# A hybrid decoder step: the SSD loop traces the next chunk's decays and scaled operands ahead of this chunk's products

## The chip, the cores and the metric

The kernel runs on one core of a Trainium2 chip. The metric is the device time of one execution in microseconds (us), the median of three runs. A TensorE matmul of 32-bit floats with 128 rows appears in the profile as two instructions, and one of the type fp32r as one.

## The reference, cut to what matters

One layer of a decoder: a prompt of 512 tokens and 8 samples of 8 tokens share the weights. A first projection feeds three groups of heads side by side (Mamba-2 SSD, mLSTM, RG-LRU), one output projection merges them, and an MLP follows. The change touches only the SSD heads of the prompt: 16 heads of 64 in 2 groups, with a state of 128, in chunks of 128 tokens that hand a state on.

```python
def ssd_chunked(x, dt, a, bm, cm, s0):
    L = math.gcd(x.shape[1], CHUNK)
    mask = causal_mask(L)[None, :, :, None, None]

    def step(s, inp):
        xc, dtc, bc, cc = inp
        cum = jnp.cumsum(dtc * a, axis=1)
        decay = jnp.exp(jnp.where(mask, cum[:, :, None] - cum[:, None, :], -jnp.inf))
        att = jnp.einsum('btgn,bsgn->btsg', cc, bc)[..., None] * decay
        xdt = xc * dtc[..., None]
        y = (jnp.einsum('btsge,bsgep->btgep', att, xdt)
             + jnp.einsum('btgn,bgepn->btgep', cc, s) * jnp.exp(cum)[..., None])
        xend = xdt * jnp.exp(cum[:, -1:] - cum)[..., None]
        s = jnp.exp(cum[:, -1])[..., None, None] * s + jnp.einsum('bsgn,bsgep->bgepn', bc, xend)
        return s, y
```

Only the two terms that hold the state s depend on the chunk before; att, xdt, xend and the decays of a chunk do not.

## The kernel before

**The main stream.** All large products are done in three passes of fp32r: a weight block of 128 x 1024 (raw) is loaded by SP's queue (L128), split by ScalarE into a high part (wh, L150) and by VectorE into a low part (wl, L151). A unit is 48 matmuls g (L163): 8 slices of the inner dimension, 3 passes, 2 halves of the 576 tokens. Loads run 4 blocks ahead of the units and splits 2 blocks ahead, with 3 buffers for raw and 3 for the split parts. At the end of a unit its result is copied out of PSUM: q, k, v of the mLSTM at L901, convolutions at L610 to L652 (conv steps r at L625 on VectorE, xbc at L650).

**The generators.** All smaller work is written as Python generators: `ssd(g)` for the two SSD groups, `mlstm`, the RG-LRU, `ada_gen` for the modulation (adap L217, adas L227, modt L228). A unit calls `slot()` after every 4 slices and at its end, and each active generator is then advanced to its next `yield`. So a `yield` sets between which g matmuls a piece of work is traced. A scheduler then orders the traced instructions on each engine, by priority in the order of tracing and by when it reckons operands and buffers free; each engine runs its order strictly from front to back. SBUF tiles (`self.T`) come from one pool of 54 buffers, small PSUM tiles (`self.P`) from 4, the PSUM pairs of units from 2.

**A chunk of ssd before** has two pieces with a `yield` behind each.

- The front (L685 to L719): TensorE computes the scores of B and C and transposes B (cb, L687, L688) and the four x tiles (xt, L690). VectorE masks the scores (cbm, L692) and scales x into xdt and xend (L697). The decays: the running sums of the chunk, broadcast over the partitions by a DMA (cumb, L666), less the row's own sum (att, 8 x L706), exponentiated by ScalarE (L708), times the masked scores (L710). From the second chunk on also the exponentials of cumb times C (ce; L713 on ScalarE, L715 on VectorE). At its end the next chunk's two cumb loads are issued.
- The back (L720 to L748): TensorE multiplies att by xdt (py, L728) and the state S by ce into the same PSUM tile (L731), and computes the state's increment (ps, L733). VectorE adds x times a constant (y, L735) and forms the new state (L742; GpSimd multiplies the old one at L739; the first chunk's is a copy by ScalarE, L744).

Behind the four chunks the same generator handles the group's sample tokens (L751 to L848). It starts with loads of cumf and cump (L759, L762) and of states s (L755); exponentials of both follow on ScalarE (L788, L790), then copies of operands on ScalarE (L800, L801) and products pc and pu (L821, L828).

Of the kernel before, what the change touches and what calls it, by code (L numbers as in the profile page):

```python
# [25 lines left out]
AF = mybir.ActivationFunctionType  # L26
# [41 lines left out]
class Kernel:  # L68
# [601 lines left out]
    def ssd(self, g):  # L670
        nc, io = self.nc, self.io
# [6 lines left out]
        for i in range(4):  # L678
            self.y[4 * g + i] = ys[i]
        mask = self.v("mask")  # L680
        S = None
        cums = [self.ssd_cum(g, 0, h) for h in range(2)]
        yield
        for c in range(4):
            tok = slice(c * 128, (c + 1) * 128)  # L685
            p1, p2 = self.P("cb"), self.P("xt")
            nc.tensor.matmul(p1[:, :128], B[:, tok], Cc[:, tok], start=True, stop=True)  # L687
            nc.tensor.transpose(p1[:, 128:256], B[:, tok], self.ident)  # L688
            for i in range(4):
                nc.tensor.transpose(p2[:, i * 128:(i + 1) * 128], xs[i][:, tok], self.ident)  # L690
            cb = self.T("cbm")
            nc.vector.tensor_tensor(cb[:, :128], p1[:, :128], mask, op=OP.mult)  # L692
            nc.scalar.activation(cb[:, 128:256], p1[:, 128:256], AF.Copy)
            hh = slice(g * 8, g * 8 + 8)
            xdt, xend = self.T("xdt"), self.T("xend")
            for dst, q in ((xdt, 64), (xend, 96)):
                nc.vector.tensor_tensor(dst[:, :512].rearrange("p (h d) -> p h d", h=8),  # L697
                                        p2.rearrange("p (h d) -> p h d", h=8),
                                        self.col1[:, c, q + g * 8:q + g * 8 + 8][:, :, None].to_broadcast([128, 8, 64]),
                                        op=OP.mult)  # L700
            att, ce = [], []
            for h2 in range(2):
                E = self.T("att")
                for h in range(4):
                    hd = g * 8 + h2 * 4 + h
                    self.eng("att").tensor_scalar(E[:, h * 128:(h + 1) * 128], cums[h2][:, h * 128:(h + 1) * 128],  # L706
                                            self.col1[:, c, hd:hd + 1], 0.0, op0=OP.add, op1=OP.min)
                nc.scalar.activation(E[:, :512], E[:, :512], AF.Exp)  # L708
                e3 = E[:, :512].rearrange("p (h t) -> p h t", h=4)
                self.eng("attm").tensor_tensor(e3, e3, cb[:, None, :128].to_broadcast([128, 4, 128]), op=OP.mult)  # L710
                att.append(E)
                if c:
                    nc.scalar.activation(cums[h2][:, :512], cums[h2][:, :512], AF.Exp)  # L713
                    c3 = cums[h2][:, :512].rearrange("p (h t) -> p h t", h=4)
                    self.eng("ce").tensor_tensor(c3, c3, Cc[:, None, tok].to_broadcast([128, 4, 128]), op=OP.mult)  # L715
                    ce.append(cums[h2])
            if c < 3:
                cums = [self.ssd_cum(g, c + 1, h) for h in range(2)]
            yield  # L719
            py, pst = self.P("py"), self.P("ps")  # L720
            for i in range(4):
                for step in range(2 if c else 1):
                    for j in range(2):
                        h = 2 * i + j
                        o = py[64 * j:64 * j + 64, i * 128:(i + 1) * 128]
                        hs = slice((h % 4) * 128, (h % 4 + 1) * 128)
                        if step == 0:
                            nc.tensor.matmul(o, xdt[:, h * 64:(h + 1) * 64], att[h // 4][:, hs], start=True,  # L728
                                             stop=not c)
                        else:  # L730
                            nc.tensor.matmul(o, S[:, h * 64:(h + 1) * 64], ce[h // 4][:, hs], start=False,  # L731
                                             stop=True)
            nc.tensor.matmul(pst, cb[:, 128:256], xend[:, :512], start=True, stop=True)  # L733
            for i in range(4):
                nc.vector.scalar_tensor_tensor(ys[i][:, tok], xs[i][:, tok], self.v("ssdd")[:, 4 * g + i:4 * g + i + 1],  # L735
                                               py[:, i * 128:(i + 1) * 128], op0=OP.mult, op1=OP.add)
            Sn = self.T("S")
            if c:
                self.eng("S").tensor_tensor(Sn[:, :512].rearrange("p (h d) -> p h d", h=8),  # L739
                                        S[:, :512].rearrange("p (h d) -> p h d", h=8),  # L740
                                        self.decb[:, hh, c][:, :, None].to_broadcast([128, 8, 64]), op=OP.mult)
                nc.vector.tensor_tensor(Sn[:, :512], Sn[:, :512], pst, op=OP.add)  # L742
            else:
                nc.scalar.activation(Sn[:, :512], pst, AF.Copy)  # L744
            S = Sn
            if c == 3:
                self.queue("ssm_p").dma_start(io["ssm_p"][g], S[:, :512])
            yield  # L748
# [8 lines left out]
        tok = slice(TP, NT)  # L757
# [13 lines left out]
        cb = self.T("cbm")  # L771
# [6 lines left out]
        xdt, xend = self.T("xdt"), self.T("xend")  # L778
# [27 lines left out]
        for i in range(4):  # L806
            for j in range(2):
                h = 2 * i + j
# [829 lines left out]
```

## Time and profile before

| what | us |
|---|---|
| median of 3 runs (lowest, highest) | 988.71 (987.87, 989.5) |
| the profiled execution, its own time | 991.71 |
| its span | 989.9 |

The mean granted TensorE clock of the profiled execution is 0.987 of full speed. The two SSD groups lie at 119 to 178 us and at 197 to 286 us of the span, their prompt chunks at 119 to 170 and 203 to 251. Rows of a timeline give the start in us, the duration in us, the engine and line, what is written and read, and in brackets how long the engine stood idle before it and what ended that. Durations of neighbours overlap a little, because an instruction is issued before the one ahead of it has drained; so the time that one takes up on its engine is read from the difference of two starts.

### The profile page before, as it was taken

To read this page: it belongs to the slowest core of one execution; us is meant where nothing else is said; L and a number is where in the kernel's file an instruction comes from. 1 tells how busy PE (TensorE), PEld (TensorE's weight loads), DVE (VectorE), ACT (ScalarE), POOL (GpSimd) and SP (SyncE) were. 2 spreads that over 40 slices of the span, in tenths; PEclk is the share of its full clock that TensorE was granted. 3 is DMA by queue.
4 is the path that set the end of the run, shared out by engine and by line. 5 is a ranking of instruction groups with operands and counts; after the bars stand their busy time and mean duration, and the time that the engine had idled before them with its cause. 6 is when DMAs were issued, how large, how long until landed. Compare 5 with 4: busy or idle time off the path is not lost.

```text
span 989.9 us, 18136 instructions
## 1 busy us (share of the span) xinstructions
PE 959.0 (97%) x7370; PEld 904.9 (91%) x7370; DVE 579.1 (59%) x1206; ACT 400.4 (40%) x741; POOL 134.9 (14%) x194
## 2 busy tenths in 40 slices
PE   8899879999899999999999999999999999999996
PEld 4789868888788889998999999999999999999996
DVE  4669878687877586557444455533553355335544
ACT  3455734554656674436222243312431144114320
POOL 2811210420331222010000000000000000000032
PEclk9999989999999999999999999999999999999998
DMA  9722263764653424434333212222222222222202
GB/s 345 294 86 79 77 177 128 236 192 140 199 196 116 151 89 138 136 124 162 109 110 108 98 65 86 85 86 77 74 85 85 86 85 83 74 79 86 86 22 96
DMA packets 51218, 119.61 MB, mean 121 GB/s; under 512 B 6956, under 2 KB 17468, under 8 KB 51136
## 3 DMA queue, kind: packets, MB, share of 16 engines
q1 hardware_dynamic: 47024, 111.06, 33.3%
q10 hardware_dynamic: 3744, 6.85, 1.8%
q8 instruction: 58, 0.95, 0.4%
q0 software_dynamic: 368, 0.55, 0.2%
q14 instruction: 24, 0.20, 0.1%
HBM read 108.68 MB, written 9.76 MB: 120 GB/s over the span
## 4 chain that ended last, share of the span: by engine, by line
PE 84%; DVE 4%; ACT 3%; DMA 2%; issue 1%; POOL 0%; POOLq 0%; DVEq 0%; SPq 0%; ACTq 0%
PE g L163 73%; PE adap L217 1%; PE g L1363 1%; PE ps L733 1%; PE py L728 1%; DMA nmb<-scr_nm 1%; PE py L731 1%; DMA ada<-ada 1%; DMA cump<-scr_cum 0%; PE lg L1129 0%; PE xt L690 0%; PE adas L227 0%; DVE wl L151 0%; PE pu L828 0%; PE pn L970 0%
## 5 line engine op out<-in xcount | busy, mean ns | idle before, releaser
L150 ACT ACTIVATE wh<-raw 128x1024 fp32r<-128x1024 f32 x123 | 130.0, 1058 | 343.8 <-PE g L163 321.3
L151 DVE TENSOR_TENSOR wl<-raw,wh 128x1024 fp32r<-128x1024 f32 x123 | 151.3, 1231 | 43.2 <-ACT wh L150 37.8
L163 PE MATMUL g<-hnh,wh 128*128 128x288 f32 x688 | 155.6, 304 | 9.7 <-ACT r L613 5.2
L163 PE MATMUL g<-hnh,wl 128*128 128x288 f32 x688 | 153.0, 301 | 0.4 <-DVE wl L151 0.4
L163 PE MATMUL g<-hnl,wh 128*128 128x288 f32 x688 | 151.7, 300 | 0.0
L163 PEld LDWEIGHTS g<-hnh,wh 128*128 128x128 f32 x688 | 112.1, 191 | 19.1 <-ACT r L613 6.3
L163 PEld LDWEIGHTS g<-hnh,wl 128*128 128x128 f32 x688 | 112.4, 191 | 2.9 <-issue 1.5
L163 PEld LDWEIGHTS g<-hnl,wh 128*128 128x128 f32 x688 | 112.5, 191 | 1.9 <-issue 1.7
L163 PE MATMUL g<-h2h,wh 128*128 128x288 f32 (+1 forms) x512 | 111.2, 298 | 0.0
L163 PE MATMUL g<-h2l,wh 128*128 128x288 f32 (+1 forms) x512 | 111.1, 298 | 0.0
L163 PE MATMUL g<-h2h,wl 128*128 128x288 f32 (+1 forms) x512 | 110.4, 297 | 0.0
L163 PE MATMUL g<-hh,wl 128*128 128x288 f32 x480 | 102.7, 295 | 0.0
L163 PE MATMUL g<-hh,wh 128*128 128x288 f32 x480 | 102.7, 295 | 0.0
L163 PE MATMUL g<-hl,wh 128*128 128x288 f32 x480 | 102.6, 295 | 0.0
L306 DVE SCALAR_TENSOR_TENSOR xr<-g,modt,xr 128x288 f32<-128x288 f32 x38 | 19.7, 518 | 141.2 <-PE g L163 141.2
L163 PEld LDWEIGHTS g<-h2l,wh 128*128 128x128 f32 x512 | 83.7, 189 | 0.0
L163 PEld LDWEIGHTS g<-h2h,wl 128*128 128x128 f32 x512 | 83.6, 189 | 0.0
L163 PEld LDWEIGHTS g<-h2h,wh 128*128 128x128 f32 x512 | 83.0, 188 | 0.1
L163 PEld LDWEIGHTS g<-hh,wl 128*128 128x128 f32 x480 | 77.0, 188 | 0.0
L163 PEld LDWEIGHTS g<-hl,wh 128*128 128x128 f32 x480 | 76.9, 188 | 0.0
L163 PEld LDWEIGHTS g<-hh,wh 128*128 128x128 f32 x480 | 76.8, 188 | 0.0
L1405 POOL TENSOR_SCALAR xr<-xr,vec 128x576 f32<-128x576 f32 (+2 forms) x8 | 15.2, 1904 | 384.8 <-ACT sqa L1237 364.4
(398 smaller groups left out, 1523.7 us busy)
## 6 DMA issues: line engine op xcount, KB each, us to landing
raw<-w SPq DMA_DIRECT2D x124, 512.0 KB, 3.5
ada<-ada SPq DMA_DIRECT2D x32, 512.0 KB, 5.1
ada<-ada SPq DMA_DIRECT2D x32, 256.0 KB, 5.8
cumb<-scr_cum SPq DMA_DIRECT2D x16, 256.0 KB, 5.8
s<-s SPq DMA_DIRECT2D x16, 256.0 KB, 4.6
ssm_s<-s ACTq DMA_DIRECT2D x16, 256.0 KB, 4.2
x<-x SPq DMA_DIRECT2D x8, 288.0 KB, 5.2
xr<-x SPq DMA_DIRECT2D x8, 288.0 KB, 3.9
```

Of the source, the lines that this page charges most:

```text
L150: nc.scalar.activation(hi, raw, AF.Copy)
L151: nc.vector.tensor_tensor(lo, raw, hi.bitcast(FT), op=OP.subtract)
L163: self.nc.tensor.matmul(pg.h[h][:m, :e], w(k), xx[:, h * HALF:h * HALF + e], start=start and n == 0, stop=stop and n == 2)
L217: nc.tensor.matmul(ps[32 * j:32 * j + 32, :256], self.cs[:, k, :], ks(k), start=k < 4, stop=k >= 4)
L306: self.nc.vector.scalar_tensor_tensor(dst[:, :HALF], pg.h[0][:, :HALF], gate[:, 0:1], x[:, :HALF], op0=OP.mult, op1=OP.add)
L728: nc.tensor.matmul(o, xdt[:, h * 64:(h + 1) * 64], att[h // 4][:, hs], start=True, stop=not c)
L731: nc.tensor.matmul(o, S[:, h * 64:(h + 1) * 64], ce[h // 4][:, hs], start=False, stop=True)
L733: nc.tensor.matmul(pst, cb[:, 128:256], xend[:, :512], start=True, stop=True)
L1363: nc.tensor.matmul(pgs[i].h[p][:, :c.stop - c.start], w(k), xs[k][x][:, c], start=k == 0 and j == 0, stop=k == 7 and j == 2)
L1405: self.eng("fin").tensor_scalar(x, x, self.v("fnw")[:, o:o + 1], None, op0=OP.mult)
```

## The change

The front becomes a function `front(c)` that returns its tiles, the back a function `back(c, S, ops)`. The order in which they are traced, `|` standing for a `yield`, was f0 | b0 | f1 | b1 | f2 | b2 | f3 | b3 and is now f0 | f1 | b0 | f2 | b1 | f3 | b2 | b3. The number of yields is the same, so what follows in the generator is traced in the same slot as before; f1 to f3 come one slot earlier and b0 to b2 one slot later. The next chunk's cumb loads are issued at the end of each front as before, and so one slot earlier. No instruction is added, removed or changed. Lines from L687 on carry numbers in the new kernel that are 1 to 16 higher (L728 is L734, L710 is L711, L735 is L741, L759 is L775); the text names lines by the kernel before.

```diff
-        S = None
-        cums = [self.ssd_cum(g, 0, h) for h in range(2)]
-        yield
-        for c in range(4):
+        cums = {0: [self.ssd_cum(g, 0, h) for h in range(2)]}
+        hh = slice(g * 8, g * 8 + 8)
+
+        def front(c):
...
             if c < 3:
-                cums = [self.ssd_cum(g, c + 1, h) for h in range(2)]
-            yield
+                cums[c + 1] = [self.ssd_cum(g, c + 1, h) for h in range(2)]
+            return cb, xdt, xend, att, ce
+
+        def back(c, S, ops):
+
+            cb, xdt, xend, att, ce = ops
+            tok = slice(c * 128, (c + 1) * 128)
             py, pst = self.P("py"), self.P("ps")
...
-            S = Sn
+            return Sn
+
+        yield
+        S = None
+        ready = [front(0)]
+        yield
+        for c in range(4):
+            if c < 3:
+                ready.append(front(c + 1))
+                yield
+            S = back(c, S, ready.pop(0))
             if c == 3:
                 self.queue("ssm_p").dma_start(io["ssm_p"][g], S[:, :512])
             yield
```

What the scheduler makes of it is seen at three places. First TensorE's order just ahead of chunk 1's first product in the first group, before (xt_1487 are chunk 1's transposed x tiles, py_1434 and py_1563 the products of chunks 0 and 1, g_1724 a unit):

```order
L690 MATMUL xt_1487<-vec,xbc_918 128x128
L690 MATMUL xt_1487<-vec,xbc_1005 128x128
L163 MATMUL g_1724<-hnl_576,wh_1458 128x288 x2
L163 MATMUL g_1724<-hnh_575,wl_1459 128x288 x2
L163 MATMUL g_1724<-hnh_616,wh_1458 128x288
L728 MATMUL py_1434<-att_1379,xdt_1368 64x128 x4
L163 MATMUL g_1724<-hnh_616,wh_1458 128x288
L163 MATMUL g_1724<-hnl_617,wh_1458 128x288 x2
L163 MATMUL g_1724<-hnh_616,wl_1459 128x288 x2
L728 MATMUL py_1563<-att_1501,xdt_1497 64x128 x2
L733 MATMUL ps_1564<-xend_1498,cbm_1494 128x512
```

and now (xt_1564 are chunk 2's, py_1631 chunk 1's product, g_1731 the same unit):

```order
L691 MATMUL xt_1564<-vec,xbc_918 128x128
L691 MATMUL xt_1564<-vec,xbc_1005 128x128
L163 MATMUL g_1731<-hnl_576,wh_1478 128x288 x2
L163 MATMUL g_1731<-hnh_575,wl_1479 128x288 x2
L163 MATMUL g_1731<-hnh_616,wh_1478 128x288 x2
L163 MATMUL g_1731<-hnl_617,wh_1478 128x288 x2
L163 MATMUL g_1731<-hnh_616,wl_1479 128x288 x2
L734 MATMUL py_1631<-att_1449,xdt_1445 64x128 x2
L739 MATMUL ps_1632<-xend_1446,cbm_1442 128x512
L737 MATMUL py_1631<-cumb_1386,S_1521 64x128 x2
```

Before, 10 g matmuls stand between chunk 1's own transposes and its product; now chunk 2's transposes are there, and chunk 1's stand further ahead: behind them come 32 g matmuls of the same unit, chunk 0's products, chunk 2's cb pair and 5 more g matmuls, none of which is in these rows.

Second, VectorE's order at the same place, before, from the last y of chunk 0 on (cbm_1494, xdt_1497, att_1501 and att_1510 are chunk 1's):

```order
L735 SCALAR_TENSOR_TENSOR y_1310<-xbc_1005,vec,py_1434 128x128
L692 TENSOR_TENSOR cbm_1494<-cb_1486,vec 128x128
L697 TENSOR_TENSOR xdt_1497<-xt_1487,col_1216 128x512
L697 TENSOR_TENSOR xend_1498<-xt_1487,col_1216 128x512
L706 TENSOR_SCALAR att_1501<-cumb_1386,col_1216 128x128 x4
L706 TENSOR_SCALAR att_1510<-cumb_1388,col_1216 128x128 x4
L650 SCALAR_TENSOR_TENSOR xbc_1560<-r_1547,r_1553 128x512
L652 SCALAR_TENSOR_TENSOR xbc_1560<-r_1547,r_1553 128x64
L151 TENSOR_TENSOR wl_1849<-raw_1590,wh_1848 128x1024
L710 TENSOR_TENSOR att_1501<-att_1501,cbm_1494 128x512
```

and now, from chunk 1's xdt on (xdt_1445, att_1449 and att_1458 are chunk 1's, y chunk 0's results):

```order
L697 TENSOR_TENSOR xdt_1445<-xt_1435,col_1216 128x512
L697 TENSOR_TENSOR xend_1446<-xt_1435,col_1216 128x512
L707 TENSOR_SCALAR att_1449<-cumb_1386,col_1216 128x128 x4
L151 TENSOR_TENSOR wl_1735<-raw_1476,wh_1734 128x1024
L707 TENSOR_SCALAR att_1458<-cumb_1388,col_1216 128x128 x4
L625 SCALAR_TENSOR_TENSOR r_1553<-r_1547,cwh,r_1553 128x600
L741 SCALAR_TENSOR_TENSOR y_1307<-xbc_752,vec,py_1506 128x128
L741 SCALAR_TENSOR_TENSOR y_1308<-xbc_840,vec,py_1506 128x128
L741 SCALAR_TENSOR_TENSOR y_1309<-xbc_918,vec,py_1506 128x128
L741 SCALAR_TENSOR_TENSOR y_1310<-xbc_1005,vec,py_1506 128x128
L711 TENSOR_TENSOR att_1449<-att_1449,cbm_1442 128x512
```

Chunk 1's scaled operands and decays stood behind chunk 0's y and now stand ahead of them; only the masking (L710, now L711) is still behind. Ahead of the second of these pieces, behind the common L228, stand only chunk 1's mask of cb, chunk 0's two maskings and a step L625.

Third, SP's queue of loads in the second group, before (nmb, c: an mLSTM head's; cumf, cump and s: the sample tokens'; raw_3195 and raw_3381: weight blocks):

```order
L128 DMA raw_3025<-w 128x1024
L666 DMA cumb_2661<-scr_cum 128x4x128
L666 DMA cumb_2663<-scr_cum 128x4x128
L908 DMA nmb_2722<-scr_nm 128x576
L911 DMA c_455_2724<-c 128x520
L911 DMA c_456_2725<-c 128x520
L128 DMA raw_3195<-w 128x1024
L237 DMA ada_2959<-ada 128x1024
L237 DMA ada_2961<-ada 128x1024
L128 DMA raw_3381<-w 128x1024
L759 DMA cumf_2963<-scr_cum 64x8x64
L762 DMA cump_2964<-scr_cum 64x4x64 x2
```

and now:

```order
L128 DMA raw_3025<-w 128x1024
L128 DMA raw_3195<-w 128x1024
L924 DMA nmb_2729<-scr_nm 128x576
L927 DMA c_459_2731<-c 128x520
L927 DMA c_460_2732<-c 128x520
L237 DMA ada_2959<-ada 128x1024
L237 DMA ada_2961<-ada 128x1024
L775 DMA cumf_2963<-scr_cum 64x8x64
L778 DMA cump_2964<-scr_cum 64x4x64 x2
L771 DMA s_495_2968<-s 128x512
L771 DMA s_496_2970<-s 128x512
```

The weight load raw_3195 now stands ahead of nmb instead of behind it, chunk 3's cumb pair further ahead, and raw_3381 no longer stands between the modulation's loads and cumf; it now follows four s loads.

More of the change, by code (lines that the diff above doesn't have):

```diff
@@ L693, in ssd @@
             nc.scalar.activation(cb[:, 128:256], p1[:, 128:256], AF.Copy)
-            hh = slice(g * 8, g * 8 + 8)
             xdt, xend = self.T("xdt"), self.T("xend")
@@ L701, in ssd @@
             att, ce = [], []
+            cu = cums.pop(c)
             for h2 in range(2):
@@ L705, in ssd @@
                     hd = g * 8 + h2 * 4 + h
-                    self.eng("att").tensor_scalar(E[:, h * 128:(h + 1) * 128], cums[h2][:, h * 128:(h + 1) * 128],
+                    self.eng("att").tensor_scalar(E[:, h * 128:(h + 1) * 128], cu[h2][:, h * 128:(h + 1) * 128],
                                             self.col1[:, c, hd:hd + 1], 0.0, op0=OP.add, op1=OP.min)
@@ L712, in ssd @@
                 if c:
-                    nc.scalar.activation(cums[h2][:, :512], cums[h2][:, :512], AF.Exp)
-                    c3 = cums[h2][:, :512].rearrange("p (h t) -> p h t", h=4)
+                    nc.scalar.activation(cu[h2][:, :512], cu[h2][:, :512], AF.Exp)
+                    c3 = cu[h2][:, :512].rearrange("p (h t) -> p h t", h=4)
                     self.eng("ce").tensor_tensor(c3, c3, Cc[:, None, tok].to_broadcast([128, 4, 128]), op=OP.mult)
-                    ce.append(cums[h2])
+                    ce.append(cu[h2])
             if c < 3:
-                cums = [self.ssd_cum(g, c + 1, h) for h in range(2)]
-            yield
+                cums[c + 1] = [self.ssd_cum(g, c + 1, h) for h in range(2)]
[3 more added lines that the diff above has]
+            tok = slice(c * 128, (c + 1) * 128)
             py, pst = self.P("py"), self.P("ps")
```

## Prediction

> **What bounds the kernel now.** I read the page's busy table first, then who waited for whom on TensorE, then the stretches around the long waits, then the timeline there.
>
> ```profile
> PE 959.0 (97%) x7370; PEld 904.9 (91%) x7370; DVE 579.1 (59%) x1206; ACT 400.4 (40%) x741; POOL 134.9 (14%) x194
> ```
>
> TensorE is busy for 97% of the span, so an edit that removes no matmul can win only what is left: its waits, and stretches in which its clock is lowered. The change moves work only around the SSD chunks (119 to 260 us), so I list the waits of that time and shortly behind it. Columns: total us, times, longest.
>
> ```profile
> PE py L728 <- DVE att L710: 6.2, 2, 5.8
> PE g L163 <- ACT v L901: 1.3, 1, 1.3
> PE pu L828 <- DVE modt L228: 1.2, 1, 1.2
> PE pc L821 <- PE g L163: 0.6, 1, 0.6
> PE pu L828 <- DVE c L1028: 0.6, 1, 0.6
> ```
>
> One wait of 5.8 us stands out: a product of a chunk (py, L728) waits for the masked decays of that chunk (att, L710). The stretches of 2 us show what it costs besides; columns: us, PE busy (instructions), granted clock, DMA share, GB/s.
>
> ```profile
> 140.00:142.00 2.00, 0.00 (x0) 0.66 0.00 0
> 142.00:144.00 2.00, 1.46 (x5) 0.50 0.44 125
> 144.00:146.00 2.00, 2.00 (x7) 0.50 0.99 307
> 146.00:148.00 2.00, 2.00 (x22) 0.63 0.54 98
> ...
> 266.00:268.00 2.00, 1.47 (x7) 0.74 0.88 299
> 268.00:270.00 2.00, 2.00 (x11) 0.50 0.80 299
> 270.00:272.00 2.00, 2.00 (x20) 0.91 0.65 195
> ```
>
> After the long wait the clock is at half until about 147.5. Lost there from 142 on: 2 x (0.50 + 0.50 + 0.37) = 2.74 us, less half of the 0.54 us in which TensorE still stood: 2.47. A second fall, at 266 to 272, costs 2 x (0.26 + 0.50 + 0.09) = 1.70.
>
> Why the wait arises is in the timeline (start, us, what; in brackets the idle time before).
>
> ```profile
> 124.72 0.51 PE L227 MATMUL adas<-vec,adarow 128*128 128x9 f32 x4
> 128.91 0.17 DVE L228 TENSOR_TENSOR modt<-adas,vec 128x18 f32<-128x18 f32 x1
> 132.08 0.83 DVE L625 SCALAR_TENSOR_TENSOR r<-r,cwh,r 128x600 f32<-128x600 f32 x1
> 135.93 1.12 DVE L735 SCALAR_TENSOR_TENSOR y<-xbc,vec,py 128x128 f32<-128x128 f32 x4 [3.02 <-PE py L728]
> 136.97 0.28 DVE L692 TENSOR_TENSOR cbm<-cb,vec 128x128 f32<-128x128 f32 x1
> 137.17 0.68 DVE L697 TENSOR_TENSOR xdt<-xt,col 128x512 f32<-128x512 f32 x1
> 137.77 0.68 DVE L697 TENSOR_TENSOR xend<-xt,col 128x512 f32<-128x512 f32 x1
> 138.37 1.65 DVE L706 TENSOR_SCALAR att<-cumb,col 128x128 f32<-128x128 f32 x8
> 139.93 0.68 DVE L650 SCALAR_TENSOR_TENSOR xbc<-r,r 128x512 f32<-128x512 f32 x1
> 140.67 1.22 DVE L151 TENSOR_TENSOR wl<-raw,wh 128x1024 fp32r<-128x1024 f32 x1
> 141.81 0.69 DVE L710 TENSOR_TENSOR att<-att,cbm 128x512 f32<-128x512 f32 x1
> 142.54 0.69 PE L728 MATMUL py<-att,xdt 128*64 128x128 f32 x4 [5.81 <-DVE att L710]
> ```
>
> VectorE first stands idle for 3.02 us for chunk 0's products, and only then starts chunk 1's front (mask, xdt, xend, decays). TensorE has five g matmuls left by then and stops at chunk 1's products, with all later g matmuls behind them in its order. One engine waits for the other, in turn.
>
> **The change, part by part.** It adds and removes no instruction; it moves. Four terms.
>
> *Term A, the long wait.* In the new order chunk 1's transposes stand right behind chunk 0's, and 32 g matmuls, chunk 0's products and chunk 2's front come before chunk 1's products. I walk both engines from the last point that both programs share: TensorE behind the adas matmuls (next start 125.05 in the trace), VectorE behind L228 (next start 128.99). These rows of the chain of waits give TensorE's durations.
>
> ```profile
> 61.08 39.55 PE g L163 x286
> 132.22 0.59 PE py L728 x8
> 132.81 1.05 PE ps L733 x2
> 239.09 0.59 PE xt L690 x4
> ```
>
> A g matmul takes 39.55 / 286 = 0.138. TensorE up to chunk 0's products: 47 of these (6.49), the cb pair (no longer than an xt group, 0.59) and xt (0.59): 132.7. On to chunk 1's products: two py groups 1.18, ps 1.05, cb 0.59, 5 g 0.69, xt 0.59, 10 g 1.38: 138.2. VectorE, by differences of the starts above: mask of cb 0.20, two L710 1.20, a convolution step 0.8, xdt and xend 1.20, four L706 0.78, wl 1.14, four L706 0.78, a step 0.8, four y 1.04, L710 0.60: 8.54, so 137.5. The decays are ready 0.7 us before TensorE asks. Walked on in the same way, chunks 2 and 3 have theirs about 3 us ahead. So 5.81 + 2.47 = 8.3 us go. The margin is thin: I put back 1.0, between the ends 0 and 8.3, nearer to 0 because the walk ends on the right side.
>
> What is late next? VectorE. These are its busy times (third figure) in stretches of 10 us, behind PE and PEld.
>
> ```profile
> 80.00:90.00 10.00, 10.00 (x78) 10.00 (x77) 9.76 (x14) 5.50 (x10) 1.21 (x5) 1.00 0.21 67
> ...
> 120.00:130.00 10.00, 10.00 (x87) 9.22 (x87) 9.12 (x22) 6.15 (x14) 1.51 (x5) 1.00 0.87 256
> 130.00:140.00 10.00, 6.74 (x52) 5.36 (x51) 6.98 (x20) 3.25 (x6) 1.06 (x1) 1.00 0.45 133
> 140.00:150.00 10.00, 7.46 (x59) 5.01 (x60) 8.41 (x21) 3.39 (x8) 1.06 (x1) 0.66 0.40 107
> 150.00:160.00 10.00, 10.00 (x89) 8.89 (x89) 7.61 (x24) 2.50 (x7) 1.06 (x1) 1.00 0.75 238
> 160.00:170.00 10.00, 10.00 (x87) 8.53 (x86) 7.99 (x19) 5.32 (x12) 1.27 (x1) 1.00 0.20 79
> ```
>
> From 120 to 170 VectorE has 40.1 us of work, and TensorE without its loss needs 50 - 8.3 = 41.7: VectorE would be 96% busy. That is tight, but from 80 to 90 it is 98% busy while TensorE never stops.
>
> *Term B, the second SSD group.* Its only wait of this kind is the rest of the first row, 6.2 - 5.8 = 0.4; there the new order has whole units between a chunk's front and its products. Gain 0.4 (0 to 0.4).
>
> *Term C, the first mLSTM head.* The 1.2 us wait for modt stands behind the nmb load; order and load stay in step with TensorE's work. Nothing (the ends are -1.2 and +1.2).
>
> *Term D, the second group's sample tokens.* The waits 1.3, 0.6 and 0.6 fall at 262 to 266 and bring on the 1.70 of low clock: 4.2 in all. They end a chain on ScalarE that began late.
>
> ```profile
> 249.14 1.33 SPq L762 DMA_DIRECT2D cump<-scr_cum  x2
> 254.44 0.42 ACT L790 ACTIVATE cump<-cump 128x256 f32<-128x256 f32 x1 [2.66 <-DMA cump<-scr_cum]
> ```
>
> ScalarE stood 2.66 us for cump. In SP's new order cumf and cump no longer stand behind the last weight load (raw), and chunk 3's products, whose tiles they reuse, stand 12 g matmuls (1.7 us) earlier. So most of the 2.66 us can go, and about as much of the waits, which sum to 2.5. Between 0 and 4.2 I take 2.5. The weight load that drops behind feeds a unit several units on; it costs nothing while that lead holds.
>
> *Moved loads.* Chunk c+1's cumb pair is issued a slot earlier, ahead of a weight load that waited for wl anyway; no price. In the second group nmb now stands behind two weight loads. Its price is bounded by these rows.
>
> ```profile
> 174.71 6.96 DMA nmb<-scr_nm
> ...
> 181.70 0.88 DVE L923 TENSOR_SCALAR nmb<-nmb,col 128x128 f32<-128x128 f32 x4 [3.77 <-DMA nmb<-scr_nm]
> ```
>
> There VectorE stood 3.77 us and TensorE 1.2 behind it. What queues behind L923 in the second group now is chunk 3's decays and chunk 2's state. Between 0 and 3.8 I take 0.7.
>
> *Sum:* 8.3 - 1.0 + 0.4 + 2.5 - 0.7 = **9.5 us**. The profiled execution took 991.7 by its own time (span 989.9 and 1.8 around it), so 982.2 there. It stands 3.0 above the median of the runs; carried to the median: 988.7 - 9.5 = **979.2**.
>
> *A rule weighed.* At 262 to 266 no single wait was longer than 1.3 us, and yet the clock fell to 0.50. The Trainium skill ("TensorE: Matmul & The Clock Gate", section "Why this matters for your kernels") advises no idle gaps over about 3 us, one idle window putting the clock back to half. This trace does not agree for short waits close together. By the page the 1.0 us put back costs itself, and the sum stays 9.5; by the row it may bring on another 1.70, and the sum is 7.8.
>
> **The rivals.**
>
> *1. VectorE keeps TensorE waiting.* For it: 96% busy, a margin of 0.7. Against it: the 98% stretch. A slip of 3 us ahead of chunk 1's products leaves a wait of 3 with 1.70 of low clock, 4.7 where I put 1.0: the gain is 5.8, **982.9**.
>
> *2. The wait only changes place.* Scheduling ahead adds five tiles (cbm, xdt, xend, two att) per group to a pool of 54, and a tile or a PSUM buffer that comes free late would hold the front back until the products again. For it: the same two engines pass work to and fro four times per group. Against it: no wait in the list of before is for such a buffer in this stretch but the 1.2 for modt. All of A and D stays: **988**.
>
> *3. Slower: nmb late in the second group.* VectorE runs in order; chunk 2's state and chunk 3's decays stand behind L923, and TensorE's later units behind the products that need them. By the walk TensorE reaches those products some 8 us after VectorE reaches L923, and the work between takes about 6, so the load may be 2 us late for nothing. To lose the 9.5 and 2 more, TensorE must wait 9 and lose 2.5 of clock, as at A: nmb must land 11 us after it is wanted. At 6.96 us per load, its issue would have to slip by 4 or more. **991**.
>
> **How the numbers follow.** Forecast 0.63, rival 1 0.19, rival 2 0.10, rival 3 0.08. A measurement of this kernel can tell about 0.2%, 2 us, from no change. Faster by more: forecast and rival 1, 0.82; the same: 0.10; slower: 0.08. The best ends give 8.3 + 0.4 + 4.2 = 12.9, so 975.8; I set the low at 975.5. The high, 986.0, takes in rival 1 with another 3 us; rivals 2 and 3 (0.18) are left out.
>
> **What would show it.** Right: no wait of py on att over 1 us, clock 1.00 from 130 to 150, VectorE's idle time for py L728 gone, adap's second pair of the group some 8 us earlier; ACT's wait for cump under 1 us, and no fall of the clock where it was at 266. Rival 1: py still waits for att, 2 to 4 us. Rival 2: that wait at another line or buffer with the same sum. Rival 3: a long idle time of VectorE before nmb L923 near 225, and py L731 waiting for S. I am wrong also if TensorE waits for wl: then weights have come too late after all.

## The result, and the profile after

The changed kernel took 983.08 us in the median of 20 runs (979.01 to 988.48), the kernel before 989.51 (987.32 to 996.23) in as many beside it: a ratio of 0.9928, 95% interval 0.9908 to 0.9949. So it is faster by 6.4 us between the medians and by 7.1 by the ratio, where 9.5 were forecast. The profiled execution took 988.14 us, with a span of 986.4, 3.5 shorter than before's. That is less than the medians say, and the cause lies ahead of the change: the first adas matmul behind the SSD's first scores, at 124.72 us before, comes 3.41 us later.

```profile
128.13 0.51 PE L227 MATMUL adas<-vec,adarow 128*128 128x9 f32 x4
...
979.66 0.43 PE L1453 MATMUL rb<-vec,col 128*128 128x128 f32 x2 [1.06 <-POOL col L1444]
```

So I compare stretches from this adas to the last rb matmul near the end: 979.66 - 128.13 = 851.53 us, against 858.38 (983.10 - 124.72) before. The change is worth **6.85 us** in the traces, in step with the medians.

In the rows PE is TensorE, PEld its weight loads, DVE VectorE, ACT ScalarE and POOL GpSimd; line numbers are those of the kernel that was profiled, and differ a little from one to the next. These are TensorE's waits between 118 and 320 us (total us, times, longest), to be held against before's list.

```profile
PE pu L844 <- DVE c L1048: 2.7, 1, 2.7
PE pt L1079 <- DVE num L1075: 0.8, 1, 0.8
PE py L734 <- DVE att L711: 0.4, 1, 0.4
PE pi L1018 <- DVE C L1000: 0.3, 1, 0.3
```

The wait of 5.8 for the decays is 0.4. The waits for v, pc and c among the second group's sample tokens, 2.5 together, are one of 2.7. The stretches of 2 us (columns as before: us, PE busy, PEld, DVE, ACT, POOL, granted clock, DMA share, GB/s) show what the clock did at both places.

```profile
140.00:142.00 2.00, 1.56 (x11) 0.88 (x9) 2.00 (x5) 1.87 (x3) 0.17 (x1) 1.00 1.08 288
...
258.00:260.00 2.00, 0.69 (x3) 0.35 (x3) 2.00 (x3) 1.95 (x4) 2.00 (x2) 1.00 0.85 250
260.00:262.00 2.00, 0.60 (x2) 0.54 (x3) 2.00 (x9) 1.97 (x6) 2.00 (x3) 0.64 0.90 336
262.00:264.00 2.00, 2.00 (x10) 2.00 (x9) 2.00 (x4) 0.00 (x0) 0.17 (x1) 0.50 1.01 382
264.00:266.00 2.00, 2.00 (x10) 2.00 (x9) 1.43 (x8) 1.30 (x6) 0.00 (x0) 0.50 0.99 265
266.00:268.00 2.00, 2.00 (x17) 1.96 (x15) 0.86 (x4) 0.81 (x5) 0.62 (x1) 0.65 0.73 266
```

At the first place the clock holds. At the second it falls, for longer than before: 2 x (0.36 + 0.50 + 0.50 + 0.35) = 3.4 us are lost to it, against 1.70, so it stood at half for 6.8 us against 3.4.

For every kernel below I work out TensorE's **loss** from such rows: a stretch's length less busy time times granted clock, summed. Each trace is first shifted so that the adas stands at 124.72. S is the stretch from adas to rb.

| kernel | loss 124-150 | 150-250 | 250-280 | S | ratio to before (95% interval) |
|---|---|---|---|---|---|
| before | 8.27 | 1.54 | 4.07 | 858.38 | |
| after | 0.44 | 1.13 | 5.71 | 851.53 | 0.9928 (0.9908 to 0.9949) |
| g0_only | 0.52 | 1.67 | 6.40 | 854.55 | 0.9951 (0.9932 to 0.9970) |
| g1_only | 7.91 | 1.67 | 4.43 | 857.20 | 0.9976 (0.9956 to 0.9996) |
| one_ahead | 1.19 | 6.87 | 7.09 | 860.08 | 1.0012 (0.9991 to 1.0033) |
| margin | 1.70 | 1.13 | 4.41 | 851.89 | 0.9940 (0.9918 to 0.9962) |
| bst1 | 0.51 | 2.01 | 3.86 | 850.56 | 0.9908 (0.9875 to 0.9940) |
| xst1 | 0.40 | 2.30 | 1.95 | 848.42 | 0.9903 (0.9866 to 0.9939) |
| both1 | 0.41 | 1.56 | 6.40 | 853.87 | 0.9910 (0.9879 to 0.9941) |
| fill_d3 | 0.78 | 1.58 | 0.54 | 850.40 | 0.9881 (0.9845 to 0.9916) |
| before_xst1 | 8.25 | 1.54 | 1.87 | 857.40 | 0.9974 (0.9945 to 1.0003) |
| xst1_s0h | 0.77 | 1.46 | 1.38 | 847.03 | 0.9847 (0.9813 to 0.9881) |

In the kernels before and after, S less the whole loss within it is 841.0 us both times: the work is the same, and the gain is loss that went. In the other kernels this rest lies between 839.6 (g1_only) and 842.6 (fill_d3, which has 1.7 us more work), so the losses place a difference in S only to 1.5 us or so. From before to after it is 7.83 at the decays and 0.41 between, less 1.64 at the sample tokens: 6.60 of the 6.85. Those 1.64 are for the most part the longer half clock of this one execution, as margin below shows.

### The profile page after: what moved, and what is told of

It is laid out like the page before. It is cut to its first block, busy times and chain, and to the rows that moved or that the text cites. A ratio compares the mean times of both kernels' runs of the same rounds, so it can differ in the third digit from the quotient of the medians.

```text
span 986.4 us, 18127 instructions
## 1 busy us (share of the span) xinstructions
PE 962.7 (98%) x7369; PEld 908.2 (92%) x7370; DVE 578.5 (59%) x1206; ACT 400.2 (41%) x741; POOL 140.6 (14%) x194
## 3 DMA queue, kind: packets, MB, share of 16 engines
q10 hardware_dynamic: 3744, 6.85, 1.8%
## 4 chain that ended last, share of the span: by engine, by line
PE 83%; DVE 4%; ACT 3%; DMA 2%; issue 1%; SPq 0%; POOL 0%; POOLq 0%; DVEq 0%; ACTq 0%
PE g L163 72%; PE adap L217 1%; PE g L1379 1%; PE py L734 1%; PE ps L739 1%; DMA cumb<-scr_cum 1%; PE py L737 1%; DMA ada<-ada 1%; PE pu L844 0%; DVE wl L151 0%; PE pn L986 0%; PE lg L1145 0%; DMA nmb<-scr_nm 0%; DVE r L625 0%; PE adas L227 0%
## 5 line engine op out<-in xcount | busy, mean ns | idle before, releaser
L150 ACT ACTIVATE wh<-raw 128x1024 fp32r<-128x1024 f32 x123 | 130.1, 1059 | 348.6 <-PE g L163 326.3
```

The costliest lines, as they stand in the source:

```text
L150: nc.scalar.activation(hi, raw, AF.Copy)
```

## The experiments

**1. Which group, which chunk, how much margin.** Three kernels trace ahead in only a part of the loop; where the condition does not hold, the order is the old one.

```diff
         for c in range(4):
-            if c < 3:
+            if not ready:
+                ready.append(front(c))
+                yield
+            if c < 3 and g == 0:
                 ready.append(front(c + 1))
                 yield
             S = back(c, S, ready.pop(0))
```

This is g0_only; g1_only has `g == 1`, one_ahead `g == 0 and c == 0`. The fourth, margin, does two of VectorE's operations of chunk 1 twice:

```diff
-            for dst, q in ((xdt, 64), (xend, 96)):
+            for dst, q in ((xdt, 64), (xend, 96)) * (2 if (g, c) == (0, 1) else 1):
```

> Only the first SSD group traces the next chunk's front ahead; the second keeps the old order. I read the stretch of the profile from the first adas matmul behind the SSD's first scores (124.72 us before, 128.13 after) to the adas at 307.87 (304.10 after): 183.15 us before, 175.97 after. Theory (the gain is the long wait in group 0; the new order of group 1 makes the sample tokens' stall worse, from 4.2 us of waits and low clock before to 5.7 after): no wait of py for att over 1 us, the stall at 262 to 270 is back as before, the stretch is 174.5, the ratio to the kernel before about 0.991. Rival (the stall in the sample tokens is worse because everything ahead of it is earlier, whatever the order of group 1): stall as after, stretch 176, ratio 0.993.

Measured: the wait for the decays goes here too (loss 0.52), but the stretch to the adas near 304 is 178.73, worse than both expectations. The sample tokens lose 6.40, more than before, though group 1 is traced in the old order; the clock is at half for 6.8 us here too. Its waits there in the timeline:

```profile
257.30 1.06 PE L840 MATMUL pc<-s,xbc 128*32 128x512 f32 x8 [1.67 <-issue]
259.67 0.76 PE L847 MATMUL pu<-xst,bst 96*128 96x512 f32 x1 [0.56 <-DVE c L1047]
261.47 0.85 PE L163 MATMUL g<-hnh,wh 128*128 128x288 f32 x2 [1.04 <-ACT v L920]
```

So the stall stands there without the new order of group 1. Measured from the first adas, TensorE comes to pc 6.1 us earlier than before (255.63 - 124.71 against 261.74 - 124.72) and v 5.0 earlier (261.47 against 266.53): TensorE has gained more than the chain behind its wait. For the 1.67 ahead of pc the profile shows no cause.

> Only the second SSD group traces the next front ahead. Theory (group 1's new order itself makes the stall of its sample tokens longer): the 5.8 us wait of py for att stays, pu waits about 2.7 us for c, the stretch from the first adas to the one at 308 is 184 to 185 (183.15 before), ratio 1.000 to 1.002. Rival (my term D: cump earlier takes 2.5 us of waits away there): 181, ratio 0.998.

Measured: the 5.8 us wait stays and pu waits 2.7 for c, as the theory has it; yet the stretch is 181.23, as the rival has it, and the ratio lies between. The losses put only tenths of a microsecond of that to a place (0.36 less low clock behind the long wait); the rest is within what the losses can't place. Neither is decided by this run.

> Only chunk 1 of the first group has its front traced ahead of chunk 0's products; chunks 2 and 3 and the second group keep the old order. Theory (one wait in one place is the whole gain): no wait of py for att over 1 us in the first group, clock 1.00 from 130 to 150, stretch 174 to 176, ratio 0.991 to 0.993. Rival (the to and fro of the two engines only moves on to chunk 2): a wait of py for att or for S of 2 us or more at 145 to 165, stretch 178 to 181, ratio 0.995 to 0.998.

Measured: both fall. The long wait is gone (1.19 of 8.27 left), and nothing is gained. New waits stand elsewhere, not at chunk 2:

```profile
161.35 0.54 PE L163 MATMUL g<-hnh,wh 128*128 128x288 f32 x2 [1.55 <-ACT r L613]
184.65 0.49 PE L847 MATMUL pu<-xst,bst 96*128 96x512 f32 x1 [0.42 <-ACT cc L843]
187.43 1.24 PE L989 MATMUL pn<-v,nmb 128*128 128x130 f32 x4 [1.47 <-DVE s L853]
...
258.82 1.93 PE L840 MATMUL pc<-s,xbc 128*32 128x512 f32 x8 [1.68 <-issue]
```

A fall of the clock comes with the second and third, and another, of 10 us, with the last; 150 to 250 loses 6.87 against 1.54, and the sample tokens 7.09 against 4.07. A gain of 7.1 is given back later, 8.4 in all. Why these new waits arise was not tried further.

> The changed kernel with 1.2 us more of VectorE work in front of chunk 1's decays (xdt and xend of chunk 1 of group 0 are computed twice). Theory (VectorE is full from 130 to 150, and the 0.4 us wait left there is where its margin ends): the wait of py for att grows by about what is added, 0.4 to 1.4 or more, the stretch 175.97 to 177, or to 178.5 if the clock falls too; ratio to the kernel before 0.994 to 0.996. Rival (VectorE has slack there that the busy time hides, since its operations overlap): wait and stretch as in the changed kernel, ratio 0.993.

Measured: py waits 1.7 instead of 0.4, one for one with the 1.2 us added. VectorE has no slack left at the decays. But the wait of 1.7 leaves the clock alone:

```profile
140.00:142.00 2.00, 0.61 (x6) 0.38 (x4) 2.00 (x6) 1.85 (x3) 0.26 (x1) 1.00 1.05 323
142.00:144.00 2.00, 1.68 (x10) 0.78 (x12) 2.00 (x5) 0.00 (x0) 0.00 (x0) 1.00 0.38 70
```

The ratio is in the span expected, the stretch is not: 175.37, 0.6 shorter than the changed kernel's and not longer. The difference lies at the sample tokens. The program is the same there and so is the wait, but the clock is at half for 3.4 us, not 6.8, and the loss is 4.41, not 5.71:

```profile
262.55 0.47 PE L844 MATMUL pu<-xst,bst 96*128 96x512 f32 x1 [2.71 <-DVE c L1048]
...
262.00:264.00 2.00, 1.45 (x10) 1.44 (x11) 2.00 (x6) 1.13 (x5) 1.33 (x2) 0.97 1.01 374
264.00:266.00 2.00, 2.00 (x10) 2.00 (x10) 1.97 (x9) 0.40 (x2) 0.00 (x0) 0.50 1.10 371
266.00:268.00 2.00, 2.00 (x14) 2.00 (x13) 1.13 (x4) 1.36 (x6) 0.00 (x0) 0.68 0.86 253
```

g1_only, with a wait of 2.71 too, lost 4.43. How long the clock stays low behind one and the same wait thus differs by execution; between these two it makes 1.3 us of loss.

**2. What holds the sample tokens.** In the changed kernel this is the timeline there.

```profile
246.32 1.23 DVE L151 TENSOR_TENSOR wl<-raw,wh 128x1024 fp32r<-128x1024 f32 x1 [3.12 <-ACT wh L150]
246.88 0.42 ACT L806 ACTIVATE cump<-cump 128x256 f32<-128x256 f32 x1
248.18 0.68 DVE L802 TENSOR_TENSOR cumf<-cumf,col 64x512 f32<-64x512 f32 x1
249.49 0.63 ACT L804 ACTIVATE cumf<-cumf 64x512 f32<-64x512 f32 x1 [2.18 <-DVE cumf L803]
...
256.87 1.06 PE L837 MATMUL pc<-s,xbc 128*32 128x512 f32 x8
257.61 2.61 DVE L819 TENSOR_SCALAR bst<-bstk,vec 96x128 fp32r<-96x128 f32 x4
258.00 4.17 POOL L847 TENSOR_TENSOR s<-s,decb 128x512 f32<-128x512 f32 x4 [4.02 <-PE pc L837]
259.52 1.06 ACT L150 ACTIVATE wh<-raw 128x1024 fp32r<-128x1024 f32 x1
260.14 1.10 DVE L1044 SCALAR_TENSOR_TENSOR c<-c,decb,pw 128x128 f32<-128x128 f32 x4
260.48 0.63 ACT L917 ACTIVATE v<-g 128x576 f32<-128x576 f32 x1
261.18 0.21 DVE L1048 TENSOR_TENSOR c<-c,pj 128x4 f32<-128x4 f32 x2
261.40 0.77 PE L844 MATMUL pu<-xst,bst 96*128 96x512 f32 x1 [2.71 <-DVE c L1048]
```

ScalarE's chain (cumf to v) ends at 261.11, VectorE's (bst, c) at 261.39. Three edits, all for the second group only, shorten one or both:

```diff
-                self.eng("bst").tensor_scalar(
+                (nc.gpsimd if g else nc.vector).tensor_scalar(
...
```

is bst1;

```diff
-                nc.scalar.activation(xst[i][32 * q:32 * q + 32, :512], xx[32 * i:32 * i + 32, :512], AF.Copy)
+                if g == 0 or i == 0:
+                    nc.scalar.activation(xst[i][32 * q:32 * q + 32, :512], xx[32 * i:32 * i + 32, :512], AF.Copy)
+                else:
+                    nc.gpsimd.tensor_copy(xst[i][32 * q:32 * q + 32, :512], xx[32 * i:32 * i + 32, :512])
```

is xst1; both1 has the two together.

> The changed kernel, with the eight small bst products of group 1's sample tokens on GpSimd instead of VectorE. In the changed kernel VectorE's second four bst took 2.61 us beside GpSimd's s, against 0.86 for the first four, and pu waits 2.7 us for the c behind them, until 261.39; but ScalarE's copies, wh and v end only at 261.11, and the next g needs v. Theory (two chains end there together): the wait goes over to g for v, 2.0 to 2.7 us, TensorE's loss from 250 to 280 us (5.7 in the changed kernel, waits and low clock) falls by less than 0.5 but for the clock's phase, ratio to the kernel before 0.992 to 0.994. Rival (the slowed bst alone makes the stall): waits there under 1 us, loss under 2, ratio 0.988 to 0.990.

Measured: the wait goes over to g for v, as the theory says.

```profile
256.55 0.63 PE L163 MATMUL g<-hnh,wh 128*128 128x288 f32 x2 [2.33 <-ACT v L917]
```

The loss fell by 1.85 rather than under 0.5: 0.4 of it is the wait, the rest a clock at half for 3.4 us instead of 6.8, the part that the expectation had left open, and that margin shows to vary without an edit there.

> The changed kernel, with three of ScalarE's six xst copies of group 1's sample tokens (0.63 us each) on GpSimd. The scheduler also moves the second pu behind 19 more g matmuls in TensorE's order. Theory (ScalarE's chain is the one that cannot be moved past): v is ready 1.9 us earlier, at about 259.2 against TensorE's 258.7, so a wait of 0.5 us or less is left, no clock falls, loss from 250 to 280 about 1 against 5.7, ratio 0.987 to 0.989. Rival (GpSimd's copies slow VectorE further, as s slowed bst, and c or wl come later): a wait of 2 us or more for VectorE, loss 4 to 6, ratio 0.992 to 0.994.

Measured: the theory, though the loss is 1.95 and not about 1. The wait for v is 0.3 and the clock holds (a 0.9 us wait of adas for s and one of 0.4 remain near 269 of the table's time); S is 3.1 us shorter than the changed kernel's; the ratio came out at 0.9903, just outside the span expected, with an interval that takes it in. The rival is right on one count that here costs nothing, since TensorE's order no longer asks there: beside GpSimd's s the four bst took 4.08 us.

```profile
251.88 4.15 POOL L850 TENSOR_TENSOR s<-s,decb 128x512 f32<-128x512 f32 x4 [1.34 <-issue]
...
252.03 4.08 DVE L822 TENSOR_SCALAR bst<-bstk,vec 96x128 fp32r<-96x128 f32 x4
```

> Both edits: group 1's bst and half of its xst copies on GpSimd. TensorE's second pu stands again right ahead of the g matmuls that wait for v. Theory (both chains must end early, and then there is nothing late): c's last reader of the PSUM slot is done near 259, v near 259.2, wait 0.5 us or less, loss from 250 to 280 about 1, ratio 0.987 to 0.989. Rival (GpSimd, now with five more pieces of work ahead of pu, becomes the late one): a wait of pu for bst or xst of 2 us or more, ratio 0.992 to 0.995.

Measured: both miss. The wait for v is 0.4, as forecast, but 10 us later TensorE waits for s twice, 1.38 for pu and 1.24 for pq; the clock falls and the loss is 6.40. In VectorE's new order those s stand behind nmb, whose four products took 3.35 us here, beside GpSimd's s from 260.26 to 264.37 (0.87 in the changed kernel), and behind a weight split. The median (ratio 0.991) suffers less than this one trace.

**3. Is the clock's fall the price of standing?** Useless work instead of a wait, in the changed kernel:

```diff
-            for j in range(4):
+            for j in list(range(4)) * (3 if (g, q) == (1, 0) else 1):
                 nc.tensor.matmul(pc[32 * j:32 * j + 32, :], Cc[:, TP + 32 * q:TP + 32 * q + 32], s0[4 * q + j][:, :512],
...
```

> The changed kernel, with the four pc products of group 1's first half done three times over, with the same operands into the same place: about 2.0 us of useless TensorE work just ahead of the place where the changed kernel's TensorE stands for 2.7 us (258.7 to 261.4) and then runs at half clock for 6 us. Because GpSimd's s waits for the last pc, it starts 2 us later and meets bst less. Theory (TensorE's clock fell because it stood): the wait shrinks to 0.7 us or less, the clock stays at 1.00 there, and the useless work costs less than the idle time it replaces: the stretch from the first adas to the last rb, 851.53 us in the changed kernel, becomes 848 to 849, ratio to the kernel before 0.988 to 0.990. Rival (the clock falls there for another reason, such as what the other engines do): half clock again for 3.4 us or more near 262 to 268, stretch 851 or more, ratio 0.993 or more.

Measured: the theory.

```profile
256.00:258.00 2.00, 2.00 (x16) 0.72 (x8) 0.96 (x4) 1.95 (x4) 0.83 (x1) 1.00 1.07 311
258.00:260.00 2.00, 1.46 (x11) 1.37 (x11) 1.92 (x4) 1.85 (x8) 2.00 (x2) 1.00 0.93 324
260.00:262.00 2.00, 2.00 (x18) 2.00 (x16) 2.00 (x5) 0.08 (x1) 2.00 (x3) 1.00 0.75 278
```

A wait of 0.54 is left, the clock stays at 1.00, and the loss there is 0.54 instead of 5.71, for 1.7 us of useless work (2.78 us for 24 pc instructions instead of 1.06 for 8). The eight bst took 0.86 for each four, since s now ran later; so part of the shorter wait is that, and the two are not separated. That standing brings the fall does not hang on this run alone: from 250 to 285 of the table's time the clock held in the four kernels whose waits add up to 1.9 us or less (this one, xst1 and, below, before_xst1 and xst1_s0h), and it fell in the eight whose waits add up to 2.3 or more. The ratio, 0.9881, is as expected. S is not (850.40 against 848 to 849): at 965 to 969 this execution lost 1.7 us more of clock where TensorE was busy throughout, of which more below. The interval of the ratio overlaps the changed kernel's, so the gain over that kernel shows in the loss and not yet in the medians.

**4. The stall without the change, and a better kernel.** before_xst1 is xst1's edit in the kernel before; xst1_s0h adds to xst1

```diff
-                self.eng("s0").tensor_tensor(s3, s3,
+                (nc.vector if g and b < 4 else nc.gpsimd).tensor_tensor(s3, s3,
...
```

> The kernel before (nothing traced ahead), with three of ScalarE's six xst copies of group 1's sample tokens on GpSimd. Theory (the stall in the sample tokens is one thing, the wait for the decays another, and each can be taken away alone): the 5.8 us wait stays, loss from 250 to 280 falls from 4.07 to 1 to 2, stretch from the first adas to the last rb 858.38 to 855.5 to 856.5, ratio 0.997 to 0.998. Rival (without the change cump lands too late, ScalarE's chain starts at 254.4 and other waits stand beside it): loss there 3.5 or more, ratio 0.999 to 1.001.

Measured: the theory on the loss, 4.07 to 1.87 with the 5.8 us wait untouched, and on the ratio, 0.9974 (its interval just takes in no change). S is 857.40 rather than 855.5 to 856.5; this trace too has the 1.7 us near the end. The two defects are separate: with the stall mended on both sides the change is worth 857.40 - 848.42 = 9.0 us, or 7.3 without that 1.7, against 6.85 with the stall in place. The medians say about the same: 0.9903 / 0.9974 = 0.9929, as with the stall.

> xst1, and GpSimd's first four s products of group 1's sample tokens on VectorE too (0.67 us each as VectorE's other operations of this shape). In xst1 VectorE's second four bst took 4.08 us beside them, and adas waited 0.9 us for the s that VectorE adds. Theory (the two engines hinder each other, so VectorE is done earlier with more work): the four bst take about 0.9 us, no wait over 0.5 us from 250 to 280, stretch 847 to 848 against 848.42, ratio 0.988 to 0.990. Rival (VectorE's 2.7 us of more work make c and wl late): waits of 1 us or more for VectorE from 255 to 272, stretch 849.5 or more, ratio 0.991 to 0.994.

Measured: the theory. VectorE does four s more and is faster at its bst.

```profile
253.59 0.86 DVE L822 TENSOR_SCALAR bst<-bstk,vec 96x128 fp32r<-96x128 f32 x4
...
255.40 2.49 DVE L850 TENSOR_TENSOR s<-s,decb 128x512 f32<-128x512 f32 x4
```

Its longest wait at the sample tokens is 0.5. The median is 978.02 us (975.73 to 979.7), the ratio 0.9847 (0.988 to 0.990 was expected). It is the fastest of all, and the only kernel whose interval lies wholly below the changed kernel's.

## Why the prediction was right, and where it was not

*Direction and mechanism* hold: the gain is the long wait and its low clock. 983.08 lies in the range, 3.9 us above the forecast; 0.8 of that is the median before, 989.51 where the forecast started from 988.7. That the sum came as near is in part luck: term D below fell outside its own ends, while A came out 0.5 better and the moved loads cost nothing.

*Term A* (7.3 after putting back 1.0) measured 7.83. Chunk 1's masked decays and its product in the new timeline:

```profile
140.21 0.68 DVE L711 TENSOR_TENSOR att<-att,cbm 128x512 f32<-128x512 f32 x1
...
141.03 0.44 PE L734 MATMUL py<-att,xdt 128*64 128x128 f32 x4 [0.44 <-DVE att L711]
```

VectorE came as walked: it let TensorE go at 141.03, or 137.6 with the 3.41 taken off, where I had 137.5. TensorE came 1.0 earlier than walked (its idle time began at 140.59, so 137.2, not 138.2), and the margin of 0.7 became a wait of 0.4. The walk had taken 0.59 for each cb and xt group, the length of a row; by the difference of starts, as VectorE was walked, an xt group takes up 0.35, and the four groups 1.3 instead of 2.4.

```profile
138.66 0.60 PE L691 MATMUL xt<-vec,xbc 128*128 128x128 f32 x4
139.01 0.51 PE L163 MATMUL g<-hnl,wh 128*128 128x288 f32 x2
```

That there is no slack is shown by margin.

*Term B* (0.4): the second group's wait for att is gone, but pt waits 0.8 for num there. *Moved loads* (-0.7): no cost. In the second group VectorE does not wait for nmb (it starts on it at 230.83 without idle time), and TensorE nowhere; the one wait for nmb, 1.50 at 178.19, is the first head's, where before it was 3.77. *Term C* (nothing): the 1.2 us wait for modt is missing in the changed kernel's trace, but bst1 and xst1, which have the same order there, show 0.9 and 1.2. It comes and goes by the execution, and the change has no part in it that the runs show.

*Term D* (2.5 gained) is **the step that failed**: the waits there, 2.5 together, became one of 2.7, so nothing was gained, and the fall of the clock near 266, whose going was named as a sign of being right, did not go. The loss is even 1.64 larger in this trace, but of that only 0.2 is waiting; the rest is the longer half clock, and margin, with the same program there, lost 4.41 against before's 4.07. The prediction said that "most of the 2.66 us can go, and about as much of the waits". The first half came true: in the timeline above ScalarE no longer waits for cump. The second did not follow, for two reasons. The next instruction on ScalarE waits 2.18 us for cumf, which VectorE had put behind a weight split. And I had counted the chain's advance as a gain on TensorE, although TensorE advances too, by term A itself. Measured from the adas, ScalarE's cumf began at 254.82 - 124.72 = 130.1 before and at 249.49 - 128.13 = 121.4 now, 8.7 earlier; TensorE's pc stood at 262.35 - 124.72 = 137.6 and stands at 256.87 - 128.13 = 128.7, 8.9 earlier. From the start of cumf to the end of v ScalarE takes 11.6 and 11.7 us. A chain that moves as far as the engine that waits for it leaves the wait where it was.

```profile
254.82 0.63 ACT L788 ACTIVATE cumf<-cumf 64x512 f32<-64x512 f32 x1
...
262.35 1.07 PE L821 MATMUL pc<-s,xbc 128*32 128x512 f32 x8 [0.61 <-PE g L163]
```

These two rows are of the timeline before. That ScalarE's chain and VectorE's both hold TensorE there is shown by bst1 (one shortened: wait 2.3) and xst1 (ScalarE shortened and TensorE's second pu moved back: 0.3). That cumf behind the split is what starts the chain late was read from the trace and not tried by itself.

*The rivals.* Rival 1: no wait of 2 us for att, though VectorE (third figure) was busy throughout from 130 to 150.

```profile
130.00:140.00 10.00, 10.00 (x82) 9.18 (x81) 10.00 (x28) 5.36 (x10) 2.88 (x3) 1.00 0.73 247
140.00:150.00 10.00, 9.56 (x85) 6.86 (x84) 10.00 (x27) 5.27 (x10) 2.15 (x2) 1.00 0.42 104
```

Rival 2, that a wait only changes place, did not come true for the decays, but it is what happened at the sample tokens, and all of one_ahead. Rival 3: not seen.

*The rule weighed.* The Trainium skill ("TensorE: Matmul & The Clock Gate", section "Why this matters for your kernels") advises against idle gaps over about 3 us. The runs put the limit lower: waits of 1.55 (one_ahead) and 1.7 (margin) left the clock at 1.00, one of 2.33 (bst1) did not, nor did 0.42 and 1.47 within some 3 us (one_ahead), 1.38 and 1.24 (both1), or 1.68 with one of 0.32 ending 1.7 us ahead of it (one_ahead). They give no sharp limit.

## What to carry to other kernels

Work traced ahead takes a wait away only as far as the chain behind the next wait gains on the engine that waits: measure every later chain against that engine's own new arrival, not in absolute time. Take the next stall in hand together with the first, since a schedule that is right for one place (one_ahead) may pay it back elsewhere. Where TensorE must stand for 2 us or more, the half clock behind the wait can cost as much again (1.7 or 3.4 us here), so that even useless matmuls in its place may pay.

## What the hardware showed besides

*The clock falls without a wait, too.* All twelve kernels are the same up to the SSD loop, and yet the adas stood between 120.61 and 128.16 us in their profiles. The changed kernel and xst1 (adas at 120.76) between 10 and 40 us, first the one and then the other:

```profile
10.00:20.00 10.00, 9.78 (x51) 6.26 (x51) 2.55 (x13) 2.29 (x6) 1.49 (x2) 0.57 1.04 394
20.00:30.00 10.00, 9.49 (x75) 5.12 (x73) 5.91 (x12) 3.33 (x7) 5.70 (x9) 0.75 1.01 373
```

```profile
10.00:20.00 10.00, 9.26 (x78) 5.71 (x77) 3.86 (x17) 3.15 (x9) 2.41 (x4) 1.00 1.04 386
20.00:30.00 10.00, 7.88 (x75) 5.05 (x76) 6.51 (x11) 4.97 (x10) 8.56 (x12) 1.00 1.04 398
```

In the first TensorE is busy and slow. Four of the twelve, margin, both1, fill_d3 and before_xst1, lost 1.7 us in the same way near the end; this is fill_d3:

```profile
964.00:966.00 2.00, 2.00 (x17) 1.96 (x17) 0.22 (x2) 0.00 (x0) 0.65 (x1) 0.96 0.00 0
966.00:968.00 2.00, 2.00 (x11) 2.00 (x11) 0.00 (x0) 0.00 (x0) 0.23 (x1) 0.50 0.00 0
968.00:970.00 2.00, 2.00 (x12) 1.66 (x11) 0.74 (x2) 0.42 (x1) 0.43 (x1) 0.69 0.00 0
```

What sets these falls off no run shows. They make most of the spread: of the changed kernel's 20 runs those at a mean clock of 0.995 took 979.0 and 980.8 us, those at 0.985 between 987.6 and 988.5 (0.010 of 980 us is 9.8 us). A single span is therefore a poor judge of a change of a few microseconds; a stretch between two matmuls that both programs share is a better one.

*VectorE's small products take turns with GpSimd's large ones.* Four bst took 0.86 us alone, 2.61 in the changed kernel and 4.08 in xst1, where all four met GpSimd's four s (4.15): about one s for each bst. The Trainium skill ("SBUF — State Buffer", section "Who interferes with whom") says that the two engines share a pair of ports, which an operation like bst (tensor_scalar) can take whole, and that the loser is blocked for the other's whole instruction; the rows agree in that they show such turns, not the ports.
